# Loads of a hybrid decoder's mixers move from SyncE's queue to ScalarE's

## The chip, the cores and the metric

The kernel runs on one core of one Trainium2 chip, as one launch. The metric is the device time of that launch in microseconds. Engines by name: TensorE (PE in the profile, with PEld for its weight loads), VectorE (DVE), ScalarE (ACT), GpSimd (POOL) and SyncE (SP), which here does nothing but issue DMAs.

## What is computed

One layer of a decoder for a prompt of 256 tokens and a group of 8 samples with 8 tokens each, in all 320 columns, in float32. `D_MODEL` is 2048. Half of the projection goes to a gated DeltaNet (8 heads of 128), half to RWKV-7 (16 heads of 64); both keep a matrix state per head. The samples start from stored states, the prompt from zero.

```python
proj = rms_norm(x, ln1_g) @ w_in                       # 2048 -> 7440 columns
o_a, gconv_new, gdn_new = gdn_mixer(proj[:, :4112], s_gconv, s_gdn, ...)
o_b, shift_new, rwkv_new = rwkv_mixer(proj[:, 4112:], s_shift, s_rwkv, ...)
x = x + concatenate([o_a, o_b]) @ w_o                  # 2048 -> 2048
f, ffn_new = conv_ffn(rms_norm(x, ln2_g), s_ffn, ffn_w_up, ffn_conv_w, ffn_w_down)   # 2048 -> 11264, 5632 -> 2048
y = rms_norm(x + f, final_g)
```

`rwkv_mixer` also multiplies by three low-rank weights (`w_b`, `a_b`, `g_b`). Each scan is done in chunks of 64 tokens with a triangular solve per chunk.

## The kernel before

All weights are streamed once from HBM in pieces of 128 x 1024 float32 (`raw`, three buffers, 512 KB each). ScalarE copies each half of a piece to a rounded high part (`whi`, four buffers), VectorE subtracts to get the low part (`wlo`, four buffers), and TensorE does three matmuls per 128 x 128 tile: high by high, high by low, low by high. This goes on through `w_in`, `w_o` (in the parts a, b, c), `w_up` and `w_dn`.

Beside the stream run the mixers: eight threads `rwkv(i)`, each for two heads, and four threads `gdn(p)`, each for two heads, started as their columns of the projection are done. Each has a thread for the samples, `rwkv_sample` and `gdn_sample`. A solve writes its matrix to HBM (`scr`, `gscr`), reads it back in another layout (`b<-scr`, `b<-gscr`), and does the same with the result (`scx`, `gscx`).

The order of all engines' instructions is written out while the program is built. `Prog.run` holds a clock for each engine, takes the threads' next operations, and emits the one that can begin first; each engine then runs its instructions in the order in which they were emitted, and waits by semaphores. A DMA is an operation of key `"S"`, whatever engine issues it: its clock advances 460 ns for each issue, and none of ScalarE's time is counted for it.

```python
op = Op("S", went + more, (out,), (in_,), lambda: (e or self.S).dma_start(out, in_))
op.lag = lag
```

All DMAs but some of the last outputs are issued by SyncE, on one queue, in the order emitted: the weights, the solves' writes and reads, the inputs' second load (`h<-xT`), the outputs, and these four loads:

- `lw<-lw`, line 1128: the low-rank weights of one `rwkv(i)`, 192 KB, 8 times;
- `b<-srw`, line 1453: the samples' RWKV state, 256 KB, 8 times, in the buffer that the thread's solve gives back just before;
- `b<-sgdn`, line 1904: the samples' DeltaNet state, 512 KB, 8 times;
- `h<-dmx` and `bi<-dmx`, line 851: rows of the mixers' output that were stored in HBM by `dmx<-b`, 160 KB, 10 and 4 times.

Line 409 is the matmul, 438 ScalarE's activation and copy, 461 VectorE's or GpSimd's product of two tensors, 507 the DMA.

Of the kernel before, what the change touches and what calls it, by code (L numbers as in the profile page):

```python
# [11 lines left out]
F32R = mybir.dt.float32r  # L12
# [7 lines left out]
P = 128  # L20
# [75 lines left out]

CFG = dict(es=0, eg=1, ln=1, bl=0, re=(7,), rg=1, gp={3: 5}, nw=(3, 4), b5=4, b4=4, b2=6, c2=9, b1=12, bi=8, raw=7, xt=2, ord='R0 R1 G0 R2 R3 Z0 G1 R4 R5 Z1 G2 R6 R7 Z2 G3 Z3', dl=1900, wr=2, l2=300, ra=3, war=1, vt=150, lw=1, lh=2, s1=9, st=6, m=60, ev=80, sp=0, cv=0, pq=1000, ug=1, sg=0, gv=1023, fs=105, pl=3000, pd=1000, pr=0.4605, ch=100, gs=1.0, hw=3400, ha=0.42, vg=350, pq2=0, lk=1, mv=126, oc=0, qn=0, aw=1.0, ls=1500, lr=600, lg=1500, hv=114, hs=125, lx=0, l3=3, hp=0, ab=0)

# [71 lines left out]
class Prog:  # L170
    def __init__(self, tc, a, ctx):
        self.tc, self.nc, self.a, self.ctx = tc, tc.nc, a, ctx
        self.uid = 0
        self.threads, self.seq = [], 0
        self.clk = dict.fromkeys("TAVGSD", 0.0)
        self.ld = self.es = 0.0
        self.port = {"V": 0.0, "G": 0.0}
        self.reads, self.writes = {k: {} for k in HELD}, {k: {} for k in HELD}
        self.shape, self.work, self.full, self.left_at = (128, 128), [], True, -1e9
        self.at, self.rd, self.bank, self.tab = {}, {}, {}, ""  # L180
        self.V, self.A, self.G, self.T, self.S = tc.nc.vector, tc.nc.scalar, tc.nc.gpsimd, tc.nc.tensor, tc.nc.sync
# [156 lines left out]

    def run(self):
        while self.threads:  # L340
            moved = True
            while moved:
# [191 lines left out]
    def wpieces(self, units):  # L534
        self.halves, self.raws = [], []
        for ap, ncol, m in units:
            step = max(m, 1024 // m * m)
            n = -(-ncol // step)
            k = ncol // m
            per = -(-k // n) * m  # L540
            at = 0
            while at < ncol:
                w = min(per, ncol - at)
                self.raws.append((ap[:, at:at + w], w))
                mid = -(-w // m // 2) * m
# [79 lines left out]
    def build(self):  # L625
# [43 lines left out]
        self.raw_s = Slots(self, wp, "raw", [P, 1024], CFG["nw"][0])  # L669
        self.hi_s = Slots(self, wp, "whi", [P, 512], CFG["nw"][1], F32R)  # L670
        self.lo_s = Slots(self, wp, "wlo", [P, 512], CFG["nw"][1], F32R)
        self.hslots = Slots(self, hp, "h", [P, NTOK], 32, F32R)
# [30 lines left out]
    def start(self):  # L703
# [4 lines left out]
        if CFG["lk"]:  # L708
            yield self.ms(G, self.zero, 0.0)
        yield self.dma(self.vec[:, 0:48], a["vec"][:, 0:48])  # L710
        self.rs = self.b1.take()
# [86 lines left out]
    def main(self):  # L798
# [44 lines left out]
        def keys(n, slots):  # L843
            for k in WO[n]:
# [275 lines left out]
    def rwkv(self, i, box):  # L1120
# [108 lines left out]
        kbc = kb_[:, :].rearrange("p (c x) -> p c x", c=RC)  # L1229
        for c0, n in ((0, 2), (2, 2), (4, 1)):  # L1230
            yield from self.want(gps)
            g = gps.take()
            for c in range(n):
                for h in range(2):
                    o = g[:, 256 * c:256 * c + 256].rearrange("p (x h t) -> p x h t", x=2, h=2)[:, :, h]
                    yield self.mm(o, kbc[:, c0 + c], ar[:, c0 + c, :, h])
            m = self.c("rmask" if c0 < 4 else "rmasks")
            m = m.rearrange("p (x t) -> p x t", x=2)
            yield self.tt(V, at[:, c0:c0 + n], g[:, 0:256 * n].rearrange("p (c x t) -> p c x t", c=n, x=2),
                    m.unsqueeze(1).to_broadcast([P, n, 2, P]), ALU.mult)  # L1240
            gps.give()
        scr = self.drams([NS, 1024], f"scr{i}")
# [6 lines left out]
        tm_ = xt_[:, 256:352]  # L1249
        yield self.dma(mt_[0:80, :], scr.unsqueeze(0).to_broadcast([GG, NS, 1024]), self.q, lag=CFG["pl"] - CFG["oc"], more=CFG["oc"])  # L1250
        yield from self.want(b2, 2)
# [41 lines left out]
        st = {"left": 2, "held": ((self.st, dec), (b5, ar_, at_), (b2, kt_, vu_, xd_))}  # L1293
        sample = self.rwkv_sample(i, st, at, ar, kt, vu, vu_, xd_, xh, yv, dec, sm)
        if CFG["es"] == 2:
# [5 lines left out]
        sx = scx.rearrange("m g (f q) i -> f (m g) q i", f=2)  # L1301
        yield self.dma(xl_[64:96, 0:256].rearrange("p (m x) -> p m x", x=32), sx[0, :, 0:8], self.q, lag=CFG["lx"])
        for f in range(2):
            yield self.dma(xd[64 + 32 * f:96 + 32 * f, :, 32 * f:32 * f + 32], sx[f], self.q)
        self.xt.give()
# [140 lines left out]

    def rwkv_sample(self, i, st, at, ar, kt, vu, vu_, xd_, xh, yv, dec, sm):
# [3 lines left out]
        w_ = self.b4.take()  # L1451
        ss = w_[:, 0:512].rearrange("p (b x) -> p b x", b=NB)
        yield self.dma(ss, self.a["srw"][i], lag=CFG["ls"])
        yield self.ms(G, w_[64:128, 512:768], 0.0)
# [22 lines left out]
        self.s1.give(rr)  # L1477
        yield from self.want(self.b4)
# [9 lines left out]
        yield from self.want(self.rB)  # L1488
        pb = self.rB.take()
        for h in range(2):  # L1490
            yield self.mm(pb[64 * h:64 * h + 64], kt[:, 4, 64 * h:64 * h + 64], vm_[:, 512 * h:512 * h + 512])
        yield self.tt(V, w_[:, 0:512], w_[:, 0:512], pb, ALU.add)
        self.rB.give()
        self.b4.give(vm_)
# [139 lines left out]
    def gdn(self, p, hd):  # L1634
# [82 lines left out]
        yield self.dma(mt_[0:80, :], scr.unsqueeze(0).to_broadcast([GG, NS, 1024]), self.q, lag=CFG["pl"] - CFG["oc"], more=CFG["oc"])  # L1717
        if CFG["mv"] & 128:
# [30 lines left out]
        for q in range(4):  # L1749
            yield self.dma(xc[32 * q:32 * q + 32], sx[q], self.q, lag=CFG["lg"])  # L1750
        yield self.vtr(tm_[:, 160:320], tm_[:, 0:160])
# [143 lines left out]
    def gdn_sample(self, p, st, kq, kw, vn, xd, qkd, ob, ssk, hd):  # L1895
        V, G = self.V, self.G
        gs, b4, s1 = self.gs, self.b4, self.s1
        yield from self.want(b4, 4 if CFG["eg"] == 0 else 3)
        ss = [b4.take(), b4.take()]
        rp_ = b4.take()  # L1900
        kr, rr = (rp_[:, o:o + 512].bitcast(F32R).rearrange("p (g x) -> p g x", g=4) for o in (0, 512))
# [11 lines left out]
        yield from self.want(s1, 1)  # L1913
        hi = s1.take()[:, :].bitcast(F32R)
        yield from self.triple(kr, kw[:, 4], hi, 1)
        yield from self.want(self.rA, 1, s1, 2)
# [11 lines left out]
        yield self.mm(pa[:, 256:384], xd[:, 4], rt)  # L1928
        yield self.pcp(rt, pa[:, 256:384], 4)
        yield self.mm(pa[:, 384:512], qkd[:, 4], rt)  # L1930
        yield self.tt(V, ob[:, 4], pa[:, 384:512], qs, ALU.add)
        self.spawn(self.gdn_square(ob, ssk, 4, hd), self.cur.prio)
        self.rA.give()
        if not CFG["gv"] & 1:
            for h in range(2):
                yield self.tt(G, sv[h], sv[h], gs["gls"][:, p, h].unsqueeze(2).to_broadcast([P, NB, P]), ALU.mult)
        yield from self.triple(rr, rt, hi, 0)
        s1.give(3)
# [142 lines left out]
```

## Time and profile before

| | us |
|---|---|
| median of 3 runs (lowest, highest) | 1716.24 (1713.74, 1716.97) |
| the profiled execution: its time | 1717.03 |
| its span, first to last instruction | 1715.2 |

The profile is of one execution. A busy TensorE means that a matmul is under way; what is missing to the span is time without any. A wait is told with what ended it. A DMA's time to landing runs from its issue. PEclk is the granted clock of TensorE, as a share of 2.4 GHz.

### The profile page before, as it was taken

To read this page: it belongs to the slowest core of one execution; us is meant where nothing else is said; L and a number is where in the kernel's file an instruction comes from. 1 tells how busy PE (TensorE), PEld (TensorE's weight loads), DVE (VectorE), ACT (ScalarE), POOL (GpSimd) and SP (SyncE) were. 2 spreads that over 40 slices of the span, in tenths; PEclk is the share of its full clock that TensorE was granted. 3 is DMA by queue.
4 is the path that set the end of the run, shared out by engine and by line. 5 is a ranking of instruction groups with operands and counts; after the bars stand their busy time and mean duration, and the time that the engine had idled before them with its cause. 6 is when DMAs were issued, how large, how long until landed. Compare 5 with 4: busy or idle time off the path is not lost.

```text
span 1715.2 us, 33329 instructions
## 1 busy us (share of the span) xinstructions
PE 1677.3 (98%) x11959; PEld 1623.2 (95%) x11959; DVE 1239.8 (72%) x3351; ACT 1021.7 (60%) x2394; POOL 178.7 (10%) x482
## 2 busy tenths in 40 slices
PE   8999999999999989999999999999999999999997
PEld 7998999889988989899999999999999999999996
DVE  8989889879998987787666666544466666665443
ACT  7886877688678856666555544433345545545442
POOL 0200000000000000231111111000011111110101
PEclk9999999999999999999999999999999999999998
DMA  6444534435353556455444444555444444444544
GB/s 231 130 133 127 170 119 141 124 122 163 114 165 100 171 167 190 138 170 163 153 150 149 148 149 151 147 153 148 152 153 151 151 148 148 150 152 144 154 145 148
DMA packets 102967, 256.53 MB, mean 150 GB/s; under 512 B 31953, under 2 KB 41425, under 8 KB 102801
## 3 DMA queue, kind: packets, MB, share of 16 engines
q1 hardware_dynamic: 102080, 253.09, 47.2%
q8 instruction: 94, 1.54, 0.4%
q10 hardware_dynamic: 720, 1.31, 0.2%
q14 instruction: 73, 0.59, 0.1%
HBM read 239.14 MB, written 15.22 MB: 148 GB/s over the span
## 4 chain that ended last, share of the span: by engine, by line
PE 79%; DVE 7%; DMA 4%; ACT 3%; issue 1%; POOL 0%; SPq 0%; DVEq 0%; ACTq 0%; POOLq 0%
PE mm L409 32%; PE rA L409 22%; PE rB L409 20%; PE g L409 5%; DVE wlo L461 2%; DMA b<-scr 2%; DVE xt L461 1%; ACT b L438 1%; DMA b<-scx 1%; DVE bi L456 1%; DVE b L461 1%; PE g L421 1%; ACT whi L438 0%; ACT L438 0%; DVE h L456 0%
## 5 line engine op out<-in xcount | busy, mean ns | idle before, releaser
L438 ACT ACTIVATE whi<-raw 128x512 fp32r<-128x512 f32 (+2 forms) x842 | 519.6, 621 | 543.2 <-PE mm L409 185.7
L461 DVE TENSOR_TENSOR wlo<-raw,whi 128x512 fp32r<-128x512 f32 (+2 forms) x842 | 573.8, 682 | 336.4 <-ACT whi L438 331.8
L409 PE MATMUL mm<-h,whi 128*128 128x320 f32 x2992 | 689.7, 314 | 0.2 <-DVE h L461 0.2
L409 PEld LDWEIGHTS mm<-h,whi 128*128 128x128 f32 x2992 | 504.3, 189 | 4.1 <-issue 2.2
L409 PE MATMUL mm<-h,wlo 128*128 128x320 f32 x1496 | 470.4, 314 | 0.3 <-DVE wlo L461 0.3
L409 PEld LDWEIGHTS mm<-h,wlo 128*128 128x128 f32 x1496 | 282.2, 189 | 3.6 <-issue 1.3
L409 PE MATMUL rB<-h,whi 128*128 128x320 f32 x1136 | 250.6, 309 | 0.0
L409 PE MATMUL rA<-h,whi 128*128 128x320 f32 x1136 | 250.6, 309 | 0.0
L409 PEld LDWEIGHTS rB<-h,whi 128*128 128x128 f32 x1136 | 189.8, 188 | 0.1
L409 PEld LDWEIGHTS rA<-h,whi 128*128 128x128 f32 x1136 | 189.8, 188 | 0.0
L409 PE MATMUL rB<-h,wlo 128*128 128x320 f32 x568 | 175.6, 309 | 0.3 <-DVE wlo L461 0.3
L409 PE MATMUL rA<-h,wlo 128*128 128x320 f32 x568 | 175.3, 309 | 0.0
L474 POOL COPY sfo<-f 128x18 f32<-128x18 f32 x88 | 61.8, 703 | 690.3 <-DVE f L461 690.3
L409 PEld LDWEIGHTS rB<-h,wlo 128*128 128x128 f32 x568 | 106.5, 188 | 0.7 <-DVE wlo L461 0.6
L409 PEld LDWEIGHTS rA<-h,wlo 128*128 128x128 f32 x568 | 106.5, 188 | 0.0
L456 DVE SCALAR_TENSOR_TENSOR f<-f,vec,f 128x336 f32<-128x336 f32 x176 | 102.9, 584 | 3.6 <-ACT f L438 0.3
L461 DVE TENSOR_TENSOR b<-b,b 80x54 f32<-80x54 f32 (+27 forms) x295 | 76.7, 261 | 9.7 <-ACT b L438 7.0
L409 PE MATMUL rA<-fx,whi 128*128 128x320 f32 x336 | 74.1, 309 | 0.0
L409 PE MATMUL rB<-fx,whi 128*128 128x320 f32 x336 | 74.1, 309 | 0.0
L409 PE MATMUL rA<-b,b 128*32 128x128 f32 (+3 forms) x488 | 55.2, 283 | 2.9 <-DMA b<-srw 2.9
L438 ACT ACTIVATE f<-f,vec 128x336 f32<-128x336 f32 x88 | 50.8, 577 | 10.3 <-DVE f L461 1.5
L409 PEld LDWEIGHTS rA<-fx,whi 128*128 128x128 f32 x336 | 56.1, 188 | 0.0
(261 smaller groups left out, 2356.0 us busy)
## 6 DMA issues: line engine op xcount, KB each, us to landing
raw<-w_up SPq DMA_DIRECT2D x176, 512.0 KB, 3.5
raw<-w_in SPq DMA_DIRECT2D x116, 512.0 KB, 4.0
raw<-w_dn SPq DMA_DIRECT2D x64, 512.0 KB, 3.6
raw<-w_dn SPq DMA_DIRECT2D x32, 384.0 KB, 3.1
raw<-w_oa SPq DMA_DIRECT2D x16, 512.0 KB, 3.9
b<-sgdn SPq DMA_DIRECT2D x8, 512.0 KB, 4.4
o_sgs<-b SPq DMA_DIRECT2D x8, 512.0 KB
raw<-w_ob SPq DMA_DIRECT2D x8, 512.0 KB, 5.2
```

The costliest lines, as they stand in the source:

```text
L409: op = Op("T", cost, (out,), (lhsT, rhs), lambda: self.nc.tensor.matmul(out, lhsT, rhs, start=start, stop=stop))
L421: op = Op("T", (1, 0.836 * self.width(in_), 107), (out,), (in_,), lambda: self.nc.tensor.transpose(out, in_, ident))
L438: lambda: self.nc.scalar.activation(out, in_, func, **kw), {AF.Exp: "E", AF.Ln: "L", AF.Silu: "S", AF.Tanh: "T"}.get(func))
L456: lambda: self.V.scalar_tensor_tensor(out, in0, scalar, in1, op0=op0, op1=op1)))
L461: lambda: e.tensor_tensor(out, in0, in1, op=op)))
L474: return self.shared(Op(self.key(e), v if e is self.V else CFG["gs"] * (120 + 3.33 * n), (out,), (in_,), lambda: e.tensor_copy(out, in_)))
```

## The change

`CFG` gets new entries, of which `aq=2` alone is not zero, empty, or as the code had it; `aq & 2` selects ScalarE for a handle `q3`, and four calls use it. `q2` (`aq & 1`) stays SyncE. Besides, in `rwkv_sample` the take of a buffer `vm_` and the two products with `bm` now stand behind the last output matmul and its copies (`rows`), where they stood ahead of them. What hangs on the other new entries (`seg`, `wf`, `rt`, `bw`, `ss`, `pv`) is not taken and is left out here.

```diff
         self.q = self.G if CFG["pq2"] else None
+        self.q2 = self.A if CFG["aq"] & 1 else self.q
+        self.q3 = self.A if CFG["aq"] & 2 else self.q
...
-                    yield self.dma(lo, self.dmx[k], lag=CFG["ls"])
+                    yield self.dma(lo, self.dmx[k], self.q3, lag=CFG["ls"])
...
-        yield self.dma(lw, self.a["lw"][i], lag=CFG["ls"])
+        yield self.dma(lw, self.a["lw"][i], self.q3, lag=CFG["ls"])
...
-        yield self.dma(ss, self.a["srw"][i], lag=CFG["ls"])
+        yield self.dma(ss, self.a["srw"][i], self.q3, lag=CFG["ls"])
...
-        yield from self.want(self.b4)
-        vm_ = self.b4.take()
-        vm = vm_[:, :].rearrange("p (h b x) -> p h b x", h=2, b=NB)
-        for h in range(2):
-            yield self.tt((self.g(4), V)[h], vm[:, h], vu[:, 4, h:h + 1].to_broadcast([P, NB, 64]),
-                    self.c("bm").unsqueeze(2).to_broadcast([P, NB, 64]), ALU.mult)
...
         yield self.mm(pa[:, 384:512], at[:, 4, 1], vu_[:, 512:640], start=False)
         yield from self.rows(yv[:, 4], pa, 384, sm[:, 4:5])
         st["o"] = 1
         self.rA.give()
...
+        if not CFG["bw"]:
+            yield from self.want(self.b4)
+            vm_ = self.b4.take()
...
+            vm = vm_[:, :].rearrange("p (h b x) -> p h b x", h=2, b=NB)
+            for h in range(2):
+                yield self.tt((self.g(4), V)[h], vm[:, h], vu[:, 4, h:h + 1].to_broadcast([P, NB, 64]),
+                        self.c("bm").unsqueeze(2).to_broadcast([P, NB, 64]), ALU.mult)
...
-            yield self.dma(sv[h], self.a["sgdn"][2 * p + h], lag=CFG["ls"])
+            yield self.dma(sv[h], self.a["sgdn"][2 * p + h], self.q3, lag=CFG["ls"])
```

## Rows read from the trace of the kernel before

**Rows 1.** The page: busy us (share of the span) x instructions.

```profile
PE 1677.3 (98%) x11959; PEld 1623.2 (95%) x11959; DVE 1239.8 (72%) x3351; ACT 1021.7 (60%) x2394; POOL 178.7 (10%) x482
```

**Rows 2.** The page: the chain that ended last, by engine.

```profile
PE 79%; DVE 7%; DMA 4%; ACT 3%; issue 1%; POOL 0%; SPq 0%; DVEq 0%; ACTq 0%; POOLq 0%
```

**Rows 3.** Windows: stretch, length, busy of each engine (instructions), clock, DMA share, GB/s.

```profile
100.00:700.00 600.00, 585.36 (x4551) 542.45 (x4550) 525.71 (x1978) 450.87 (x1355) 41.81 (x129) 0.99 0.46 141
...
775.00:1700.00 925.00, 925.00 (x6307) 924.68 (x6307) 563.52 (x1058) 442.36 (x751) 95.72 (x281) 1.00 0.48 150
```

**Rows 4.** Waits from 30 to 780 us: total us, times, longest.

```profile
PE rA L409 <- DMA b<-srw: 2.9, 1, 2.9
...
PE g L409 <- DMA b<-scx: 1.4, 1, 1.4
...
ACT whi L438 <- DMA raw<-w_in: 2.4, 3, 1.2
```

**Rows 5.** Windows around three waits of TensorE, columns as above.

```profile
600.00:610.00 10.00, 8.72 (x84) 8.27 (x83) 8.97 (x51) 4.27 (x10) 0.00 (x0) 1.00 0.76 208
...
330.20:333.70 3.50, 3.50 (x16) 3.37 (x16) 1.70 (x7) 2.54 (x8) 0.00 (x0) 0.51 0.85 294
620.80:623.70 2.90, 0.00 (x1) 0.00 (x1) 1.46 (x4) 0.99 (x2) 0.00 (x0) 1.00 0.59 219
623.70:630.70 7.00, 7.00 (x31) 7.00 (x32) 4.48 (x21) 2.63 (x13) 0.00 (x0) 0.51 0.17 32
```

**Rows 6.** Timeline of SyncE's issues: start us, us, what.

```profile
613.83 0.64 SPq L507 DMA_DIRECT2D b<-gscr  x1
614.52 0.45 SPq L507 DMA_DIRECT2D bi<-dmx  x1
615.02 1.38 SPq L507 DMA_DIRECT2D h<-xT  x3
616.44 0.43 SPq L507 DMA_DIRECT2D b<-srw  x1
```

**Rows 7.** The chain, 588 to 640 us: start us, us, what.

```profile
615.65 0.63 PE g L409 x16
...
616.44 7.21 DMA b<-srw
```

**Rows 8.** DMA issues: count, KB each, median us to landing.

```profile
b<-srw SPq DMA_DIRECT2D x8, 256.0 KB, 4.3
...
bi<-dmx SPq DMA_DIRECT2D x4, 160.0 KB, 4.0
```

**Rows 9.** Timeline of ScalarE: in brackets its idle time before, and what ended it.

```profile
616.30 0.38 ACT L438 ACTIVATE b<-g 32x256 f32<-32x256 f32 x1 [0.67 <-PE g L409]
...
621.75 0.47 ACT L438 ACTIVATE bi<-bi 128x320 fp32r<-128x320 f32 x1 [2.47 <-DMA bi<-dmx]
...
625.64 0.80 ACT L438 ACTIVATE b<-rA 64x128 f32<-64x128 f32 x3 [2.91 <-PE rA L409]
```

**Rows 10.** Timeline of VectorE at the same place.

```profile
622.24 0.49 DVE L461 TENSOR_TENSOR h<-h,mm 128x320 f32<-128x320 f32 x1 [3.74 <-DMA h<-xT]
```

**Rows 11.** Timeline of TensorE: two waits.

```profile
603.27 0.98 PE L409 MATMUL g<-c 128*64 128x128 f32 x13 [1.28 <-DVE c L456]
...
623.70 1.91 PE L409 MATMUL rA<-b,b 128*128 128x64 f32 x8 [2.93 <-DMA b<-srw]
```

**Rows 12.** Issues of two moved loads: duration ns min/median/max, first and last start us.

```profile
L507 SPq DMA_DIRECT2D b<-srw x8: 423/431/1437, 139.7 to 704.2; - x8
...
L507 SPq DMA_DIRECT2D h<-dmx x10: 327/404/535, 602.6 to 733.1; - x10
```

**Rows 13.** SyncE's own waits over the span: total us, times, longest.

```profile
SPq L507 <- DVE lh L461: 3.2, 1, 3.2
```

**Rows 14.** Timelines of VectorE and TensorE near the mixers' end.

```profile
716.12 1.29 DVE L461 TENSOR_TENSOR b<-b,cst 128x512 f32<-128x512 f32 x2
...
725.44 0.33 PE L421 MATMUL g<-cst,b 128*128 128x128 f32 x1 [0.93 <-ACT b L438]
```

More of the change, by code (lines that the diff above doesn't have):

```diff
@@ L339, in run @@
     def run(self):
+        turns = list(CFG["seg"])
         while self.threads:
+            while turns and self.clk["T"] >= 1e3 * turns[0][0]:
+                CFG.update(turns.pop(0)[1])
             moved = True
@@ L1229, in rwkv @@
         kbc = kb_[:, :].rearrange("p (c x) -> p c x", c=RC)
[L1230 to L1233, printed above, removed]
-                for h in range(2):
[L1235 to L1241, printed above, removed]
+        if CFG["rt"]:
+            for c0, n in ((0, 4), (4, 1)):
+                yield from self.want(gps, 2)
+                two_ = (gps.take(), gps.take())
+                for c in range(n):
+                    for h in range(2):
+                        z = slice(64 * h, 64 * h + 64)
+                        yield self.mm(two_[h][:, 128 * c:128 * c + 128].rearrange("p (x t) -> p x t", x=2), kb[z, c0 + c].rearrange("p x t -> p (x t)"), ar[z, c0 + c, :, h])
+                m = self.c("rmask" if c0 < 4 else "rmasks")
+                m = m.rearrange("p (x h t) -> p h x t", x=2, h=2)
+                for h in range(2):
+                    yield self.tt(V, at_[:, :].rearrange("p (x c h t) -> p h c x t", c=RC, x=2, h=2)[:, h, c0:c0 + n], two_[h][:, 0:128 * n].rearrange("p (c x t) -> p c x t", c=n, x=2),
+                            m[:, h].unsqueeze(1).to_broadcast([P, n, 2, 64]), ALU.mult)
+                gps.give(2)
+        else:
+            for c0, n in ((0, 2), (2, 2), (4, 1)):
+                yield from self.want(gps)
+                g = gps.take()
+                for c in range(n):
+                    for h in range(2):
+                        o = g[:, 256 * c:256 * c + 256].rearrange("p (x h t) -> p x h t", x=2, h=2)[:, :, h]
+                        yield self.mm(o, kbc[:, c0 + c], ar[:, c0 + c, :, h])
+                m = self.c("rmask" if c0 < 4 else "rmasks")
+                m = m.rearrange("p (x t) -> p x t", x=2)
+                yield self.tt(V, at[:, c0:c0 + n], g[:, 0:256 * n].rearrange("p (c x t) -> p c x t", c=n, x=2),
+                        m.unsqueeze(1).to_broadcast([P, n, 2, P]), ALU.mult)
+                gps.give()
@@ L1293, in rwkv @@
         st = {"left": 2, "held": ((self.st, dec), (b5, ar_, at_), (b2, kt_, vu_, xd_))}
-        sample = self.rwkv_sample(i, st, at, ar, kt, vu, vu_, xd_, xh, yv, dec, sm)
+        sample = self.rwkv_sample(i, st, at, ar, kt_, kt, vu, vu_, xd_, xh, yv, dec, sm)
         if CFG["es"] == 2:
@@ L1445, in solve, with rwkv_sample @@
             yield self.tt(V, x[:, 0:q, j + 1:32], x[:, 0:q, j + 1:32], t, ALU.subtract)
-    def rwkv_sample(self, i, st, at, ar, kt, vu, vu_, xd_, xh, yv, dec, sm):
+    def rwkv_sample(self, i, st, at, ar, kt_, kt, vu, vu_, xd_, xh, yv, dec, sm):
         V, G = self.V, self.G
         ident = self.c("ident")[0:64, 0:64]
-        yield from self.want(self.b4)
+        yield from self.want(self.b4, 1 + CFG["bw"])
         w_ = self.b4.take()
+        vm_ = self.b4.take() if CFG["bw"] else None
         ss = w_[:, 0:512].rearrange("p (b x) -> p b x", b=NB)
-        yield self.dma(ss, self.a["srw"][i], lag=CFG["ls"])
+        yield self.dma(ss, self.a["srw"][i], self.q3, lag=CFG["ls"])
         yield self.ms(G, w_[64:128, 512:768], 0.0)
@@ L1477, in rwkv_sample @@
         self.s1.give(rr)
-        yield from self.want(self.b4)
-        vm_ = self.b4.take()
-        vm = vm_[:, :].rearrange("p (h b x) -> p h b x", h=2, b=NB)
-        for h in range(2):
-            yield self.tt((self.g(4), V)[h], vm[:, h], vu[:, 4, h:h + 1].to_broadcast([P, NB, 64]),
-                    self.c("bm").unsqueeze(2).to_broadcast([P, NB, 64]), ALU.mult)
+        if CFG["ss"] & 1:
+            scs = self.drams([P, 2, P], f"scs{i}")
+            for n, z in enumerate((kt_, vu_)):
+                yield self.dma(scs[:, n], z[:, 512:640], self.q)
         yield self.mm(pa[:, 384:512], at[:, 4, 1], vu_[:, 512:640], start=False)
@@ L1487, in rwkv_sample @@
         self.rA.give()
[L1488 to L1493, printed above, removed]
+        if not CFG["bw"]:
+            yield from self.want(self.b4)
+            vm_ = self.b4.take()
+        if CFG["ss"] & 1:
+            sr = scs.rearrange("(x q s t) w c -> x s t q (w c)", x=2, q=2, s=4)
+            for x in range(4):
+                for n in range(2):
+                    o = 32 * x + 8 * n
+                    yield self.dma(vm_[o:o + 8, 0:512].rearrange("p (q y) -> p q y", q=2), sr[n, x], self.q, lag=CFG["lz"])
+        else:
+            vm = vm_[:, :].rearrange("p (h b x) -> p h b x", h=2, b=NB)
+            for h in range(2):
+                yield self.tt((self.g(4), V)[h], vm[:, h], vu[:, 4, h:h + 1].to_broadcast([P, NB, 64]),
+                        self.c("bm").unsqueeze(2).to_broadcast([P, NB, 64]), ALU.mult)
+        if CFG["ss"] & 1:
+            for x in (0, 2):
+                yield from self.want(self.rA, 1, self.rB)
+                two = (self.rA.take(), self.rB.take())
+                for q in range(2):
+                    for h in range(2):
+                        for y in range(2):
+                            z, o = vm_[32 * (x + y):32 * (x + y) + 16], 256 * q + 64 * h
+                            yield self.mm(two[y][64 * h:64 * h + 64, 64 * q:64 * q + 64], z[:, o:o + 64], z[:, o + 128:o + 192])
+                for y in range(2):
+                    sb = ss.rearrange("p (q s) x -> p s q x", q=2)[:, x + y]
+                    yield self.tt(V, sb, sb, two[y][:, 0:128].rearrange("p (q x) -> p q x", q=2), ALU.add)
+                self.rA.give()
+                self.rB.give()
+        else:
+            yield from self.want(self.rB)
+            pb = self.rB.take()
+            for h in range(2):
+                yield self.mm(pb[64 * h:64 * h + 64], kt[:, 4, 64 * h:64 * h + 64], vm_[:, 512 * h:512 * h + 512])
+            yield self.tt(V, w_[:, 0:512], w_[:, 0:512], pb, ALU.add)
+            self.rB.give()
         self.b4.give(vm_)
@@ L1897, in gdn_sample @@
         gs, b4, s1 = self.gs, self.b4, self.s1
-        yield from self.want(b4, 4 if CFG["eg"] == 0 else 3)
+        strips = CFG["ss"] & 2
+        yield from self.want(b4, 4 if CFG["eg"] == 0 else 2 if strips else 3)
         ss = [b4.take(), b4.take()]
-        rp_ = b4.take()
-        kr, rr = (rp_[:, o:o + 512].bitcast(F32R).rearrange("p (g x) -> p g x", g=4) for o in (0, 512))
+        if not strips:
+            rp_ = b4.take()
+            kr, rr = (rp_[:, o:o + 512].bitcast(F32R).rearrange("p (g x) -> p g x", g=4) for o in (0, 512))
         sv = [t[:, :].rearrange("p (b x) -> p b x", b=NB) for t in ss]
         for h in range(2):
-            yield self.dma(sv[h], self.a["sgdn"][2 * p + h], lag=CFG["ls"])
+            yield self.dma(sv[h], self.a["sgdn"][2 * p + h], self.q3, lag=CFG["ls"])
         yield from self.want(b4)
@@ L1912, in gdn_sample @@
                 yield self.cp((V, G)[x], dst, kq[h][:, 4, x].rearrange("p (g j t) -> p g j t", g=2, t=8))
-        yield from self.want(s1, 1)
-        hi = s1.take()[:, :].bitcast(F32R)
-        yield from self.triple(kr, kw[:, 4], hi, 1)
+        if not strips:
+            yield from self.want(s1, 1)
+            hi = s1.take()[:, :].bitcast(F32R)
+            yield from self.triple(kr, kw[:, 4], hi, 1)
+        else:
+            scs = self.drams([P, 2, P], f"gscs{p}")
+            sr = scs.rearrange("(a s t) w c -> s t a (w c)", a=4, s=4)
+            yield self.dma(scs[:, 0], kw[:, 4], self.q)
         yield from self.want(self.rA, 1, s1, 2)
@@ L1936, in gdn_sample @@
                 yield self.tt(G, sv[h], sv[h], gs["gls"][:, p, h].unsqueeze(2).to_broadcast([P, NB, P]), ALU.mult)
+        if strips:
+            s1.give(2)
+            b4.give(km_)
+            yield from self.want(b4)
+            z_ = b4.take()
+            for x in range(4):
+                yield self.dma(z_[32 * x:32 * x + 8, :].rearrange("p (a y) -> p a y", a=4), sr[x], self.q, lag=CFG["lz"])
+            for x in (0, 2):
+                yield from self.want(self.rA, 1, self.rB)
+                pb = (self.rA.take(), self.rB.take())
+                for a in range(4):
+                    for y in range(2):
+                        z = z_[32 * (x + y):32 * (x + y) + 8, 256 * a:256 * a + 256]
+                        yield self.mm(pb[y][:, 128 * a:128 * a + 128], z[:, 0:128], z[:, 128:256])
+                for a in range(4):
+                    for y in range(2):
+                        h, b = a // 2, 4 * (a % 2) + x + y
+                        yield self.stt(sv[h][:, b], sv[h][:, b], gs["gls"][:, p, h, b:b + 1], pb[y][:, 128 * a:128 * a + 128])
+                self.rA.give()
+                self.rB.give()
+            for h in range(2):
+                yield self.dma(self.a["o_sgs"][2 * p + h], sv[h])
+            b4.give(3)
+            self.release(st)
+            return
         yield from self.triple(rr, rt, hi, 0)
```

23 lines of the change are left out of this document (13 added, 10 removed).

## The prediction

> **What bounds the kernel now.** The page's busy line comes first: TensorE is busy 98% of the span, VectorE 72%, ScalarE 60% [rows 1]. The reader should take from it that at most some 38 us of the span are without a matmul (1715.2 less 1677.3), so that nothing off TensorE can be worth more than these and what a lower clock costs. The chain that ended last agrees: 79% TensorE, 4% DMA, 3% ScalarE [rows 2]. The windows then say where: from 775 to 1700 us TensorE has no gap at all and stands at the full clock; no load that moves is issued there, so that stretch stays as it is [rows 3]. The change lives in the mixers. Between 100 and 700 us TensorE misses 600 - 585.4 = 14.6 us, and ScalarE is busy 450.9 of 600 us [rows 3].
>
> Next the waits: which of the missing microseconds is ended by a load that moves? Of the four kinds only one appears under TensorE, the state of RWKV (`srw`), once, with 2.9 us; the other DMA wait, 1.4 us on `scx`, is on a tile whose load stays [rows 4]. So the prize is one place, and I read it closely.
>
> There TensorE stands empty from 620.8 to 623.7 us. Its clock, at full speed until then, is granted at 0.51 for the next 7.0 us, which is the lower level, 1.2 of 2.4 GHz, and is back at 1.00 after that [rows 5]. Seven microseconds at half speed lose 7.0 x 0.49 = 3.4 us of work. The stall therefore costs 2.9 + 3.4 = 6.3 us, more than twice what the wait row says.
>
> Why was the load late? It was issued at 616.44, in a crowd on SyncE [rows 6], and landed 7.21 us later [rows 7]; the median of its kind is 4.3 [rows 8]. It wasn't issued late: 16 matmuls read its buffer until 616.28 [rows 7]. What stands ahead of it on the queue is `b<-gscr` at 613.83 [rows 6]. The two loads behind that one show the same delay: `bi<-dmx`, issued at 614.52, releases ScalarE at 621.75, and `h<-xT`, issued at 615.02, releases VectorE at 622.24, both 7.2 us after issue [rows 6, 9, 10], where `bi<-dmx` has a median of 4.0 [rows 8]. So the lateness belongs to the queue behind `b<-gscr`. The change takes two of these three loads off that queue.
>
> **The change part by part.** *The state at 616 us.* Its buffer comes free no earlier than now. ScalarE is in a copy until 616.68 [rows 9], so I put the issue at 616.7, 0.3 us later than SyncE's. On an empty queue it would take the median, 4.3 us; if nothing is gained, 7.2. I take 5.0, near the clear one, because what was ahead is on another queue while its bytes still have to be moved at the same time. It then lands at 621.7; TensorE comes for it at 623.70 - 2.93 = 620.77, and waits 0.9 instead of 2.9: 2.0 us saved. The clock: a wait of 1.4 us (on `scx`) was followed by a stretch at 0.51 of 3.5 us, one of 1.28 us by none [rows 5, 11]. 0.9 lies below both, so I take it that the fall goes: 3.4 us saved. What is late next? `h<-xT` stays on SyncE behind `b<-gscr`, so VectorE remains held to 622.24 [rows 10]; and the ScalarE copies that follow (0.80 us from 625.64, [rows 9]) were partly hidden under matmuls at half speed and no longer are. For both I give back 1.0 us, a little over that one row, between nothing and the whole of what was saved on the wait, 2.0. Together -4.4; bounds 0 and -6.3.
>
> The skill has a rule that speaks against this gain: the Trainium skill, "DMA: Bandwidth & Descriptors", section "Issuing engines are not separate DMA queues", says that all issuers end on the same 16 DMA engines and that a second issuer saves only the sequencer's time of issue. Taken alone it would leave the state's landing at 623.65, make this term 0 and the sum +0.4. The three 7.2 us landings behind one transfer rather speak for a delay by order on one queue, and the same page, section "Queues, rings and completion order", has each DMA engine take turns between queues that have work. No row of before shows two busy queues, so which of the two wins isn't settled by this trace.
>
> *ScalarE's issues.* 38 issues move: 8 `lw`, 8 `srw`, 8 `sgdn`, 14 from `dmx`. On SyncE one holds the sequencer 0.40 to 0.43 us [rows 12]; on ScalarE I use the same, 38 x 0.42 = 16 us. Where ScalarE waits for TensorE anyway, this is free; elsewhere what stands behind it (weight halves for TensorE, the mixers' copies) comes 0.4 us later. Weight halves are made up to four ahead, which hides such a step; a copy of a mixer is hidden only by the slack in TensorE's order. The trace gives a price: ScalarE holds 3% of the chain [rows 2], 51 us, and as 775 to 1700 us is all TensorE, these lie in the other 790 us, 6.5% of them. 16 x 0.065 = 1.0. Below: 0. Above: every issue that falls in ScalarE's busy time goes to the end, 16 x 450.9/600 = 12 us [rows 3]. I take +1.0, because chain and waits agree that ScalarE is seldom last.
>
> *Waits on ScalarE.* A load must wait for its buffer, and this wait now stands in ScalarE's order. On SyncE the one long wait that I find for a moved load is 3.2 us, `lw` for the split of the weights before it [rows 13]. As the planner places each load where it believes the buffer free, I price this at nothing and make it a rival.
>
> *The order in a sample's RWKV thread.* The diff also moves the two products with `bm` behind the last output matmul. They take 1.29 us on VectorE for the last pair, whose chain over ScalarE and GpSimd ends in TensorE's wait of 0.93 at 725.44 [rows 14]. Done earlier by up to 1.3 us it saves up to that wait; as the order of all later instructions is planned anew, it could also lose as much. I take -0.6, bounds -1.3 and +1.3.
>
> *SyncE.* It loses 16 us of issues and weights stand behind fewer loads. Weight halves waited 2.4 us for weights [rows 4], on ScalarE, ahead of TensorE; price 0, bound -2.4. The loads that aren't waited for (`sgdn`, `lw`) gain nothing by landing sooner.
>
> Sum: -4.4 + 1.0 - 0.6 = -4.0. The profiled execution took 1717.03 (span 1715.2 and 1.8 around it), which gives 1713.0. The median is 0.8 below that execution, so 1712.2, 0.24% under 1716.24. What a measurement of this kernel can tell from no change is about 0.2%, 3.4 us.
>
> **Rivals.** *The landing doesn't change* (chance 0.20): the DMA engines are the limit, the state lands at 623.65 as before, and ScalarE pays. -0.6 + 1.0 = +0.4: 1716.6. For it: the two queues' bytes are the same. Against: the three landings above.
>
> *More goes than one stall* (0.15): the wait and fall at 620.8 wholly (-6.3), the wait at 725.44 wholly (-1.3), and the wait on `scx` at 328.8 with its 3.5 us at half speed shrinks as the new order shifts it (-1.4): with +0.5 for ScalarE -8.5, 1707.7. Against: three things must go well.
>
> *Slower* (0.19): ScalarE held. A load whose buffer isn't free stops ScalarE with all that it owes TensorE. The place is where two mixers overlap, between the first state load at 139.7 us and the last at 704.2 [rows 12]; the price is that of the issues fully on the path, +12, against the saving of 5.0: +7.0, 1723.2. It decides from 5 us of such holds on, a third of the 16. For it: 3.2 us of wait in one row [rows 13], and a hold that empties TensorE as `scx` did also brings a stretch at the lower clock. Against: ScalarE idles 149 of 600 us [rows 3].
>
> **How the numbers follow.** The forecast has 0.46; its own range is 1708.5 to 1715.5, of which about six tenths lie more than 0.2% below the median. Faster: 0.29 + 0.15 = 0.44. Same: 0.17 of the forecast and 0.17 of the first rival, 0.34. Slower: 0.19 + 0.03 = 0.22. The range runs from the better side of the second rival to near the slower one's centre: 1706 to 1721.
>
> **What would show it.** Right: 38 loads issued on ScalarE's queue; the seventh of the eight state loads, at about 616 us, lands under 5.5 us after its issue; no TensorE wait on `srw` above 1.4 us; clock 1.00 from 620 to 640; ScalarE's busy time unchanged and its idle time in the mixers smaller by some 16 us. Wrong: a landing of 7 us on the new queue; new TensorE waits on ScalarE between 100 and 700 us of together over 4 us; a new stretch at half clock.

## The result, and the profile after

The changed kernel takes 1726.22 us (median of 5 runs, 1720.77 to 1730.77) against 1716.24 before (5 runs): a ratio of 1.0051, 95% interval 1.0037 to 1.0065. It is slower by about 9 us, where 4 us less were forecast; it also lies above the range (1706 to 1721) and above the rival "Slower" (1723.2). The profiled execution of after is the slowest of its five, 1730.77 us with a span of 1728.9, so its single rows are an upper picture of the loss.

The page of after: busy time, and the chain that ended last, which answer to [rows 1, 2].

```profile
PE 1684.8 (97%) x11959; PEld 1626.0 (94%) x11959; DVE 1242.4 (72%) x3351; ACT 1021.8 (59%) x2394; POOL 175.9 (10%) x482
...
PE 75%; DVE 9%; DMA 4%; ACT 4%; issue 2%; POOL 1%; SPq 0%; ACTq 0%; DVEq 0%; POOLq 0%
```

TensorE's busy time grew by 7.5 us with the same 11959 instructions (matmuls at a lower clock last longer), and its idle time from 37.9 to 44.1 us. Together that is the 13.7 us between the spans. The windows say where. The first two answer to [rows 3]; the others are stages of the mixers (length, busy of each engine, clock, DMA share, GB/s):

```profile
100.00:700.00 600.00, 579.88 (x4428) 533.30 (x4428) 517.89 (x1954) 445.04 (x1338) 37.78 (x119) 0.99 0.46 140
775.00:1700.00 925.00, 924.19 (x6301) 923.77 (x6301) 572.30 (x1071) 448.84 (x766) 100.08 (x288) 1.00 0.48 150
...
645.00:690.00 45.00, 43.10 (x303) 38.67 (x301) 30.04 (x128) 27.97 (x95) 2.24 (x6) 0.85 0.51 150
...
673.00:686.70 13.70, 13.70 (x101) 12.06 (x102) 4.52 (x13) 7.10 (x22) 2.03 (x4) 0.50 0.53 167
```

From 775 us on next to nothing changed (0.8 us). From 100 to 700 us TensorE now misses 20.1 us instead of 14.6, and it ran at its lower level (1.2 GHz) for 13.7 us from 673.0 on, behind a wait of 1.90 us. The waits from 30 to 780 us, which answer to [rows 4] (total us, times, longest):

```profile
ACT whi L443 <- DMA raw<-w_oa: 9.3, 4, 5.3
...
PE g L414 <- DVE b L494: 5.0, 6, 1.9
...
PE rA L414 <- DMA b<-srw: 0.7, 2, 0.4
```

Before, the second of these was:

```profile
PE g L409 <- DVE b L489: 1.3, 3, 0.6
```

The wait that the prediction went for is gone: 2.9 us became 0.7. In its place ScalarE waits 9.3 us for pieces of `w_oa`, for which it didn't wait before, and TensorE 5.0 us on VectorE's transposes of a solve. (Lines of the code after stand 5 below those of before: 414 is the matmul, 443 ScalarE's copy, 466 VectorE's product.)

### The profile page after: what moved, and what is told of

Its sections match the earlier page's. It is cut to its first block, busy times and chain, and to the rows that moved or that the text cites. A ratio compares the mean times of both kernels' runs of the same rounds, so it can differ in the third digit from the quotient of the medians.

```text
span 1728.9 us, 33305 instructions
## 1 busy us (share of the span) xinstructions
PE 1684.8 (97%) x11959; PEld 1626.0 (94%) x11959; DVE 1242.4 (72%) x3351; ACT 1021.8 (59%) x2394; POOL 175.9 (10%) x482
## 4 chain that ended last, share of the span: by engine, by line
PE 75%; DVE 9%; DMA 4%; ACT 4%; issue 2%; POOL 1%; SPq 0%; ACTq 0%; DVEq 0%; POOLq 0%
PE mm L414 29%; PE rA L414 21%; PE rB L414 20%; PE g L414 4%; DVE wlo L466 3%; DVE xt L466 2%; ACT b L443 2%; DMA b<-scr 1%; DMA b<-scx 1%; DVE b L466 1%; DVE bi L461 1%; ACT whi L443 1%; ACT L443 1%; PE g L426 1%; ACT s L443 1%
## 5 line engine op out<-in xcount | busy, mean ns | idle before, releaser
L414 PEld LDWEIGHTS rB<-fx,whi 128*128 128x128 f32 x336 | 56.1, 188 | 0.0
```

What stands on the lines that cost most here:

```text
L414: op = Op("T", cost, (out,), (lhsT, rhs), lambda: self.nc.tensor.matmul(out, lhsT, rhs, start=start, stop=stop))
```

## The experiments

Every kernel was timed against the kernel before on the same chip; ratios are with 95% intervals.

### The two halves of the change

**Only the queue**: after, with the two products put back where they were. All engines then run before's order, but for 38 issues on ScalarE.

```diff
+        yield from self.want(self.b4)
+        vm_ = self.b4.take()
+        ... the two products with bm, ahead of the last output matmul
         yield self.mm(pa[:, 384:512], at[:, 4, 1], vu_[:, 512:640], start=False)
```

> Only the four kinds of load go to ScalarE's queue; the products with bm stay where they were, so every engine's other instructions keep the order of before. Theory H (ScalarE pays: its issues and the loads' waits for buffers stand in its order): most of the loss is here, 1721 to 1727 us, +5 to +10. Theory O (the loss is the new order that follows from moving the products in the samples' RWKV thread): 1710 to 1717, and TensorE's wait on srw near 620 us under 1.4 us. My forecast's term for the state would then be seen: clock 1.00 from 620 to 640 us.

**Only the order**: after, with `aq=0`, so that all 38 loads stay on SyncE.

> The order of the changed kernel, instruction by instruction on TensorE, VectorE and GpSimd, with the four loads back on SyncE. H: 1714 to 1718 us, no change. O: 1721 to 1727.

Measured: the queue alone 1.0026 (1.0014 to 1.0038), the order alone 1.0045 (1.0033 to 1.0057). Both cost. The part that I had put at -0.6 us is the larger loss, some 7.7 us. The queue alone, at 1717.80 us, lies under the 1721 to 1727 of theory H. The two add up to 0.71%, against 0.51% for both at once; the intervals don't exclude that they simply add.

The order alone also takes the wait on the state away, with every load on SyncE. From 585 to 735 us TensorE waits for it only this long, at 717 us:

```profile
PE rA L414 <- DMA b<-srw: 0.8, 1, 0.8
```

So the smaller wait in after isn't evidence for the queue. In after the seventh state load is issued at 639.76 us, 23 us later than before, and lands 4.17 us after its issue.

### Is it ScalarE's time, or the queue?

**Loads stay on SyncE, ScalarE issues a dummy for each.** It stores 512 bytes, 4 from each partition, to scratch: the time of an issue without its load.

```diff
+        def both():
+            self.uid += 1
+            self.A.dma_start(self.drams([P, 1], f"pad{self.uid}"), self.zero)
+            return self.S.dma_start(out, in_)
```

> The order and the queues of before; but where each of the 38 loads is issued on SyncE, ScalarE issues a store of 512 bytes to a scratch of its own in HBM, whose source is ready from the start. So ScalarE spends the time of 38 issues (about 0.34 us each, 13 us) without a wait for a buffer, and no load changes queues. The store is additional work and feeds nothing. If H holds by the time of issue alone: as e1, +5 to +10 us. If H holds by the waits for buffers: 0 to +3 us. My forecast's price of issue was +1.0.

**The 38 loads on GpSimd's queue**, before's order: `self.q3 = self.G` (and one condition more, so that the planner counts them as before).

> As e1, but GpSimd issues the loads, on its queue; ScalarE and SyncE are both relieved. GpSimd's own instructions are few (10% busy), its order is otherwise that of before. H: ScalarE's cost is gone, 1709 to 1717 us, unless loads stand behind GpSimd's waits and come late. If a second queue itself is the cost (its loads and the weights take from one another): as e1.

The dummy gave 1.0764 (1.0746 to 1.0782): 131 us, ten times what 38 issues of 0.33 us take. So it doesn't measure what it was made for. Waits in its trace (total us, times, longest) show that the tiny stores were slow and that other loads became late too:

```profile
ACT whi L443 <- DMA pad<-zero: 17.6, 2, 12.9
...
ACT lh L443 <- DMA lw<-lw: 15.1, 5, 4.9
DVE h L466 <- DMA h<-xT: 14.2, 1, 14.2
...
SPq L516 <- DMA pad<-zero: 14.4, 4, 4.9
```

The last row is SyncE's, which waits for stores whose data nobody reads. In these programs every load has a semaphore, a counter that tells of its landing. The traces show that SyncE's and ScalarE's loads share eight of them in turn, while GpSimd's have eight of their own, and that an issue waits until the earlier load on its semaphore has landed. A slow store thus holds later issues on both engines. The clock is the other part: its mean is 0.961 in these runs, 72 us of the span by the missing share, against 8 before.

GpSimd's queue gave 1.0002 (0.9992 to 1.0011). Its trace overturns one of the prediction's readings. The timeline around the seventh state load:

```profile
608.99 0.54 POOL L512 DMA_DIRECT2D b<-srw  x1
...
614.67 0.69 PE L414 MATMUL g<-b,b 32*32 32x32 f32 x16
...
619.70 1.00 PE L414 MATMUL rA<-b,b 128*128 128x64 f32 x8
```

The order of all other work is before's, yet the state is issued 5.7 us ahead of the 16 matmuls that, as I had it, were still reading its buffer. It lands in time, and TensorE doesn't wait for it at all. The buffer had been free; SyncE came to the load late.

### Which loads cost on ScalarE?

**Only `srw` and `dmx` (22), only `sgdn` (8), only `lw` (8)** on ScalarE, before's order; the others get `self.q` again:

```diff
-        yield self.dma(lw, self.a["lw"][i], self.q3, lag=CFG["ls"])
+        yield self.dma(lw, self.a["lw"][i], self.q, lag=CFG["ls"])
```

> Before's order on every engine; of the 38 loads only the 8 state loads of RWKV (srw) and the 14 stored rows (dmx) are issued by ScalarE, lw and sgdn stay on SyncE. Theory A (what costs in the queue-only kernel is lw, whose buffer ScalarE waits for at 69 us, and sgdn, whose megabyte now starts beside the solve's scratch store at 508 us): both losses go, 1.3 and some 4.8 us of the 0.26%, and the state's gain stays: ratio 0.997 to 1.000, no half-clock stretch at 523 us, no TensorE wait on srw above 1.5 us. Theory B (each issue that ScalarE makes costs, whatever it loads): 22 of 38 issues keep 22/38 of the loss, 1.0015.

> Before's order; only the 8 loads of the DeltaNet's state (sgdn, 512 KB each) are issued by ScalarE. Theory A: the wait of the solve on its scratch (b<-gscx) at 520 us appears with the half-clock stretch behind it, as in the queue-only kernel: +4 to +6 us there, ratio 1.002 to 1.004. The state's stall at 620 us stays as before. Theory B (issues): 8 of 38, 1.0005. Rival C (the stall at 520 us of the queue-only kernel came from a shift that the other loads made): 1.000 and no wait there.

> Before's order; only the 8 loads of the low-rank weights (lw) are issued by ScalarE. Theory A (ScalarE stands in the wait for the buffer of lw at 69 us, with the weight halves behind it): TensorE 1.3 us later from 79 us on, a gap of 1.7 us on ScalarE ended by the split lh; ratio 1.0005 to 1.0015, and the rest of the queue-only kernel's 0.26% comes from lw and sgdn together. Rival (lw costs nothing, all comes from sgdn, of which the run of its own gave 0.08%): 1.000 and no shift at 79 us.

Measured: 1.0002 (0.9994 to 1.0011), 1.0008 (0.9997 to 1.0018) and 1.0008 (0.9999 to 1.0018). The 22 loads together cost nothing that can be measured, so a cost for each issue (theory B) falls. `sgdn` and `lw` each lose about 1.4 us, neither surely by itself; the three make 0.18% of the 0.26%, and the rest lies within the intervals. For `sgdn` that is under the 1.002 to 1.004 of theory A.

The 22 loads hide a gain of 1.2 us and a loss of 1.9. With `srw` on ScalarE's queue the state lands 6.1 us after its issue at 615.43, where 5.0 were forecast. TensorE waits 1.7 us for it instead of 2.9 (theory A had at most 1.5), and a new gap stands ahead of it:

```profile
PE g L414 <- issue: 1.9, 1, 1.9
PE rA L414 <- DMA b<-srw: 1.7, 1, 1.7
```

The timeline at the gap:

```profile
608.12 0.33 ACTq L512 DMA_DIRECT2D h<-dmx  x1
608.50 0.47 ACT L443 ACTIVATE h<-h 128x320 fp32r<-128x320 f32 x1 [2.01 <-DMA gscr<-b]
609.00 0.49 DVE L466 TENSOR_TENSOR h<-h,h 128x320 fp32r<-128x320 f32 x1 [1.48 <-ACT h L443]
...
610.79 0.66 PE L414 MATMUL g<-b,b 32*32 32x32 f32 x16 [1.90 <-issue]
```

ScalarE stands at the issue at 608.12 until an earlier `h<-dmx`, issued at 603.72, has landed on the same semaphore at 608.10. Its copy, VectorE's products and TensorE follow late. The queue-only kernel has the same gap with 2.52 us, before hasn't. No run gives ScalarE's loads semaphores of their own, so what this is worth in all isn't measured.

The price of `lw` is seen in the run of its own. ScalarE's timeline (in brackets the idle time before, and what ended it):

```profile
69.22 0.34 ACTq L512 DMA_DIRECT2D lw<-lw  x1
69.61 0.38 ACT L443 ACTIVATE et<-g 128x256 f32<-128x256 f32 x1 [1.74 <-DVE lh L466]
...
70.04 0.41 PE L414 MATMUL g<-xa,lh 128*128 128x320 f32 x1 [1.42 <-ACT et L443]
```

ScalarE stands until VectorE has split the weights that lie in the buffer, and TensorE waits for the copy behind. The matmuls of the stream are 1.27 us later from 79 us on, and about as much later in the queue-only kernel and in the change, but not in the one with GpSimd's queue. It is the wait in which SyncE stood before [rows 13], at no cost there. In this run 0.8 us of the delay is left at 200 us and 0.2 at 300, so it isn't shown that the whole of it reaches the end.

`sgdn` meets the solve's scratch. In the queue-only kernel:

```profile
508.14 1.08 ACTq L512 DMA_DIRECT2D b<-sgdn  x2
509.25 0.33 SPq L512 DMA_DIRECT2D gscx<-b  x1
514.90 1.27 SPq L512 DMA_DIRECT2D b<-gscx  x3
...
522.17 0.34 DVE L494 STREAM_TRANSPOSE b<-b 128x160 f32<-128x160 f32 x1 [2.13 <-DMA b<-gscx]
...
522.94 0.41 PE L414 MATMUL g<-b,blk 128*128 128x320 f32 x1 [1.91 <-DVE b L466]
```

Before, at the same place:

```profile
509.02 0.33 SPq L507 DMA_DIRECT2D gscx<-b  x1
...
513.53 1.27 SPq L507 DMA_DIRECT2D b<-gscx  x3
```

A megabyte starts 1.1 us ahead of the 80 KB that the solve writes and reads back (2.95 us ahead before). The read can be issued only 5.65 us after the write, against 4.51 before. VectorE waits 2.13 us, where it didn't wait before, TensorE 1.91, and 6.8 us at half clock follow: the matmuls behind it are 4.8 us later against before than those ahead of it. With `sgdn` alone on ScalarE the wait of VectorE was 0.74 and no fall of the clock followed. So the delay is there in both, but the size of it is not fixed.

### Why the state's earlier landing gave nothing

**`b<-gscr` on GpSimd**, none of the 38 loads moved: the transfer behind which the three landings of 7.2 us stood is off the queue.

```diff
-        yield self.dma(mt_[0:80, :], scr.unsqueeze(0)..., self.q2, ...)
+        yield self.dma(mt_[0:80, :], scr.unsqueeze(0)..., self.G, ...)
```

> Before's order, none of the 38 loads moved; instead the 4 loads b<-gscr, behind which the three landings of 7.2 us stood at 613 to 624 us, are issued by GpSimd. Theory L (what stands behind b<-gscr on one queue lands late): bi<-dmx, h<-xT and srw land in 4 to 5 us, TensorE's wait on srw falls from 2.9 to under 1, ratio 0.997 to 0.999. Rival (the bytes are the limit, whatever the queue): the state lands 6 to 7 us after its issue, the wait stays above 2, ratio 1.000.

**Only `srw` on GpSimd** (8 loads), everything else as before.

> Before's order; only the 8 state loads of RWKV (srw) are issued by GpSimd, everything else as before. Theory I (the state was issued late, because SyncE came to it late, not because its buffer was taken): issued at about 609 to 612 us, landed by 619, TensorE's wait of 2.9 us and the half clock behind it go, nothing else moves: ratio 0.997 to 0.999. Rival (the 16 DMA engines are full from 604 to 620 us, and what the state gains the stored rows or x lose): the wait goes, another of 1 to 3 us takes its place, 0.9995 to 1.0005.

The first gave 1.0021 (1.0012 to 1.0030), and theory L fell; it is also worse than its rival, which had 1.000. Its timeline:

```profile
611.20 0.62 POOL L512 DMA_DIRECT2D b<-gscr  x1 [16.71 <-DMA b<-scx]
611.70 1.33 SPq L512 DMA_DIRECT2D h<-xT  x3
613.08 0.63 SPq L512 DMA_DIRECT2D b<-srw  x1
...
622.73 0.99 PE L414 MATMUL rA<-b,b 128*128 128x64 f32 x7 [3.27 <-DMA b<-srw]
```

The chain of the same kernel (start us, us, what):

```profile
613.08 9.61 DMA b<-srw
```

With nothing of `b<-gscr` on its queue the state lands 9.61 us after its issue. The rows of before that the prediction lacks are these windows (the DMA share is the last column but one):

```profile
604.00:620.00 16.00, 15.46 (x146) 14.48 (x143) 14.26 (x56) 9.68 (x23) 0.00 (x0) 1.00 0.95 272
621.40:623.70 2.30, 0.00 (x1) 0.00 (x1) 1.46 (x4) 0.99 (x2) 0.00 (x0) 1.00 0.53 206
```

The 16 DMA engines were busy 95% of the time from 604 to 620 us: stored rows, `b<-gscr`, `h<-xT`, `w_oa` and the state are one crowd. Three landings of equal lateness behind one transfer look the same whether a queue or the engines are full. The Trainium skill, "DMA: Bandwidth & Descriptors", section "Issuing engines are not separate DMA queues", has the rule that I weighed and set aside: all issuers share the 16 engines. The 9.61 us on a separate queue agree with it.

A crowd on all engines isn't the whole of it, though: in the last 2.3 us of TensorE's wait the share is 0.53. The trace has the times of a load's semaphore updates, sixteen for most loads. Twelve of the state's came within 4.91 us of its issue, the last four between 6.97 and 7.21. Every load that follows `b<-gscr` closely shows this split, in before and in this run (here the state's twelve come within 5.59, its last four from 8.37 to 9.61). `b<-gscr` itself reads its source four times over (`to_broadcast([GG, NS, 1024])` with `GG` 4), and its last four updates come 7.21 to 7.66 us after its issue. So the late parts seem to be those that share four of the sixteen engines with `b<-gscr`, on whatever queue it stands. The trace doesn't name the engine of an update, and no run spreads `b<-gscr` over all engines, so this is a reading and not shown by an experiment.

The second run issues the state at 598.47 us, 18 us before SyncE did, and the wait for it vanishes. It gave 1.0010 (0.9999 to 1.0020): no gain, and above both expectations, though its interval reaches the rival's. What TensorE waits for between 600 and 640 us there:

```profile
PE g L414 <- DVE c L461: 2.1, 1, 2.1
PE rA L414 <- DVE s L474: 1.0, 1, 1.0
PE rB L414 <- ACT s L443: 0.5, 1, 0.5
```

Before, the first of these was 1.28 us [rows 11] and the other two weren't in the list; `b<-scr`, on which VectorE's solve waits ahead of it, landed 8.27 us after its issue there and 7.41 before. So of the 2.9 us some 0.8 went into the solve ahead, which now lands later, and 1.5 into waits behind the state. That is the rival of that run in kind. The first of these waits is also followed by 3.4 us at half clock, from 605.6 on. What takes the rest isn't settled. With all 38 loads on GpSimd the wait was gone too, at 1.0002.

The clock term had a fault of its own. The kernel with only the products moved (next part) keeps before's loads; TensorE waits 2.8 us for the state in its trace, and the clock doesn't fall. Its window right behind that wait, to be held against the last of [rows 5]:

```profile
623.70:630.70 7.00, 6.90 (x52) 6.67 (x53) 6.65 (x32) 4.72 (x18) 0.00 (x0) 1.00 0.22 54
```

With only `sgdn` moved, TensorE waits 2.5 us at this place, and about half of those 7 us are at half clock:

```profile
622.80:629.80 7.00, 6.99 (x42) 6.99 (x43) 6.00 (x28) 3.87 (x17) 0.00 (x0) 0.76 0.20 50
```

So a wait of this length is followed by 0, 3.4 or 7 us at half clock, and the 3.4 us of work that the prediction put on it are what one execution lost. In its 100 later runs, on four chips, the kernel before has medians from 1713.93 to 1715.06 us; the profiled 1717.03 was a dear one.

### What the order costs

**Only the place of the products**: before's plan, and the two products of each pair emitted behind the last output copies. Nothing else changes its place.

```diff
+            late.append(op.fn)
+            op.fn = lambda: None
...
+        rows[-1].fn = lambda last=rows[-1].fn: [f() for f in (last, *late)]
```

> All loads on SyncE; before's order on every engine, but the two products with bm of each of the eight RWKV pairs stand behind the last output matmul's two copies, as in the change (only those 16 instructions change their place, 20 lines on VectorE). Theory P (the products' place costs: the update of the state starts later): 1.003 to 1.005, as in the order-only kernel. Theory R (what costs is the new plan that the edit calls forth, with w_oa late behind other loads on SyncE): 1.000, between 0.999 and 1.001; my term for it in the prediction was -0.6 us.

**Another plan for no reason**: before's code with `ls=1490`, and with `ls=1600`, where it had 1500 (the planner's idea of these loads' landing).

> Before's code and queues with one number of the planner changed by less than 1%: the landing time that it believes of these loads is 1490 instead of 1500 ns. It orders the instructions anew (944 lines of difference on TensorE, 494 on ScalarE; the order-only kernel has 678 and 273). Theory R: plans that differ for no reason of substance differ by several us, so this one lies away from 1.000 by up to 0.5%, either side. Theory P: it has no reason to differ, 0.999 to 1.001.

> Before's code and queues, the planner's believed landing time 1600 instead of 1500 ns: another plan, with 1006 lines of difference on TensorE and 567 on ScalarE. If plans of this size of difference scatter about a mean above the tuned one: 1.001 to 1.005, like the first of them (1.0022). If the first was chance and plans scatter about before's: anywhere from 0.998 to 1.002.

The products' place alone: 1.0016 (1.0005 to 1.0026). In its trace TensorE now waits for them at the last pair, where before it waited later for ScalarE ([rows 14]):

```profile
716.31 1.28 DVE L466 TENSOR_TENSOR b<-b,cst 128x512 f32<-128x512 f32 x2
717.14 1.58 PE L414 MATMUL rB<-b,b 128*64 128x512 f32 x4 [0.90 <-DVE b L466]
```

The wait has moved rather than grown: from 714 to 727 us TensorE waits 0.90 and 0.33 us now, 0.93 and 0.33 before. Where the 0.16% arises isn't settled. The two meaningless plans: 1.0022 (1.0014 to 1.0031) and 1.0012 (1.0003 to 1.0020). Both theories hold in part: the place costs, and a plan that differs for no reason costs as much. If place and plan simply add, the 0.45% of the order alone are 0.16% of place and some 0.3% of new plan, above the two meaningless ones; no run tests that they add.

**What in this plan is late?** In after, SyncE issues a piece of `w_oa` at 622.21 us and the next at 630.06, with three loads `h<-xT` between, the third of them only at 629.63; ScalarE waits 5.35 us, until 630.72, for the first of these pieces, which lands 8.40 us after its issue. So I put the `h<-xT` loads on GpSimd: `yield self.dma(x, a["xT"][:, n], self.G)` in the changed kernel. And **the 38 loads on GpSimd in the changed kernel's plan**: `self.q3 = self.G`.

> The changed kernel with one thing more: the 16 loads h<-xT of the mixers' stretch, which hold SyncE while their buffers are taken and the weights w_oa behind them, are issued by GpSimd; plan and all other orders as in the changed kernel. Theory R (in the new plan w_oa stands behind these loads): ScalarE's waits on w_oa, 9.3 us in the changed kernel, fall below 3, TensorE's gaps at 628 to 638 us go, ratio 1.001 to 1.003. Rival (w_oa waits for its own buffer or the bytes): waits on w_oa stay above 6 us, 1.005.

> The changed kernel with its 38 loads on GpSimd's queue instead of ScalarE's, its plan kept. If the plan is the cause: 1.004 to 1.005, as the order-only kernel (1.0045). If ScalarE as issuer is: the 0.26% of the queue-only kernel go, 1.002 to 1.003.

The first gave 1.0070 (1.0057 to 1.0083): worse than the change, and than both expectations. Its timeline of ScalarE and TensorE:

```profile
629.47 1.15 ACT L443 ACTIVATE whi<-raw 128x512 fp32r<-128x512 f32 x2 [9.23 <-DMA raw<-w_oa]
630.15 0.90 PE L414 MATMUL g<-h,whi 128*128 128x320 f32 x2 [4.98 <-ACT whi L443]
```

Its chain has the load for which they wait:

```profile
617.61 11.75 DMA raw<-w_oa
```

And the window around it:

```profile
612.00:628.00 16.00, 13.17 (x90) 12.91 (x88) 10.93 (x32) 5.15 (x11) 7.39 (x18) 1.00 0.98 281
```

`w_oa` is issued 4.6 us earlier than in after, yet takes 11.75 us and lands only 1.3 us earlier: twelve `h<-xT` from GpSimd are under way at the same time, on engines that are 98% busy. My theory that it stood behind these loads on SyncE falls; here too the DMA engines are the limit. And `b<-gscr` is there again: it is issued 0.7 us ahead of that piece in both kernels, and the piece's last four updates come late in both, 8.14 to 8.40 us after issue in after (the other twelve by 6.31) and 10.60 to 11.75 here (by 8.20).

The second gave 1.0106 (1.0091 to 1.0122), outside both expectations: TensorE waits 4.14 us at 723.09 for a copy of a stored row that landed late, and 2.54 at 483.69. Its mean granted clock is 0.9885, which by the missing share of the span is 19.9 us against 8.3 before, so well over half of its loss is clock. The plan is thus not a cost by itself that an idle issuer would lay bare; what it costs depends on when each load is issued. Which of its transfers would have to stand elsewhere stays open.

## Why the prediction was wrong, point by point

**What bounds the kernel**: right. 775 to 1700 us is all but unchanged, and the loss arose in the mixers.

**The state at 616 us**, -4.4: the gain didn't come; with only the state moved, to GpSimd, the kernel takes 0.10% more (-0.01 to +0.20%), and with `srw` and `dmx` on ScalarE 0.02% more (-0.06 to +0.11%). In before's order ScalarE's queue brought the wait from 2.9 to 1.7 us, where 0.9 was forecast, and its issues opened a gap of 1.9 us ahead of it. That the wait is gone in after is luck, for the new order alone does it. Three steps failed. "It wasn't issued late: 16 matmuls read its buffer until 616.28": two rows that follow each other in the chain were taken for cause and effect; GpSimd issued it at 598.47. "So the lateness belongs to the queue behind `b<-gscr`": with `b<-gscr` off that queue it took 9.61 us; in before the DMA engines were 95% busy from 604 to 620 us. `b<-gscr` does seem to be what delays it, but on the engines that they share. And the 3.4 us for the clock came from one execution: the same wait elsewhere was followed by no fall or by half of it. The rival "The landing doesn't change", with 0.20, had the limit right in kind, the DMA engines and not the queue; its 1716.6 had no loss by the order.

**ScalarE's issues**, +1.0: not contradicted. One takes 0.33 to 0.34 us, and 22 of them, with what the moved loads gained, changed the time by between -0.06 and +0.11%.

**Waits on ScalarE**, priced at nothing: the step that failed is "As the planner places each load where it believes the buffer free, I price this at nothing". Its own row of 3.2 us [rows 13] was the very wait, and it costs TensorE 1.42 us at 70 us, of which 0.2 is left at 300 us in that trace. It lies at 69 us, ahead of the stretch named in the rival "Slower". The prediction also thought of buffers alone: ScalarE's issues wait for a shared semaphore too, behind which TensorE has the gaps of 1.9 and 2.5 us at 610 to 620 us.

**What the moved loads do to others**: not in the sum at all. The sentence "The loads that aren't waited for (`sgdn`, `lw`) gain nothing by landing sooner" asked only what they gain. `sgdn` on its own queue delayed the solve's scratch, up to 4.8 us in one execution.

**The order in a sample's RWKV thread**, -0.6 with bounds of 1.3: the largest miss, about +7.7 us by the order-only kernel. The step that failed is "Done earlier by up to 1.3 us it saves up to that wait; as the order of all later instructions is planned anew, it could also lose as much". Only the last pair was looked at, where TensorE's waits moved and came to the same sum, and the new plan was given the bound of one wait. Plans that differ for no reason cost 0.12 and 0.22%. Which instruction of the new plan is late, and why it costs more than those, stays open.

**SyncE**, 0: nothing was gained; weights waited longer in the mixers, not less.

**The clock**: "a new stretch at half clock" was named as a sign of error, and it came. Over its five runs the changed kernel has a mean granted clock of 0.9932, before 0.9951 to 0.9953 in its later runs. Span times the missing share is 11.7 us against 8.1 to 8.4: about a third of the loss is a lower clock, and the rest is left to TensorE's waits. Which wait brings a fall isn't shown.

## What to carry to other kernels

Before a late landing is put down to a queue, read the DMA share of that very window (0.95 here), and look at which parts of the load are late: another queue or an earlier issue may only choose which transfer is late. Moving a load to an engine that computes moves its waits there too, for the buffer and for the semaphore; price them from the rows of the engine that issued it before. In a kernel whose order is planned, an edit that calls for a new plan has the spread of plans as its uncertainty (here 0.1 to 0.2% for plans of no meaning), and the part of the diff that looks smallest can decide.

## What was not expected of the hardware

Thirty-eight stores of 512 bytes, 4 bytes from each of 128 partitions, on ScalarE's queue made the kernel 131 us slower, about 3.4 us each, though an issue took 0.33 us; about half of it is the lower clock. And the clock doesn't follow from the last wait alone: 2.8 us without a matmul were followed by no fall in one execution, 2.5 by 3.4 us at half speed in another, 2.9 by 7 us in a third, 1.90 by 13.7 us in a fourth.
